# Products of two experts' weight tiles queued directly one behind the other on TensorE

## The chip, the cores and the metric

The kernel runs on one core of a Trainium2 chip. The metric is the time of one execution on the device in microseconds (us), lower is better. The kernel before takes 4514.1 us in the median of three runs (4512.46 to 4516.55).

## What is computed

The reference is two transformer blocks behind each other on 512 tokens of width 1024. The first block (a state-space branch, dilated and memory attention, and a PEER layer) and the token mixers of the second are not touched by the change. The second block has two layers, and each ends with a mixture of experts: of 32 experts each token is sent to two, chosen inside one of four groups, and each expert is a SwiGLU of hidden width 512.

```python
def hier_moe(h, w_grp, b_grp, w_exp, b_exp, w1, w3, w2):
    ...
    def expert_block(args):
        tok_b, w_b, e = args
        xb = t[tok_b]
        hid = jax.nn.silu(xb @ w1[e]) * (xb @ w3[e])
        return (hid @ w2[e]) * w_b[:, None].astype(t.dtype)
```

## The kernel before

The expert stage of a layer (`moe`) gives each expert 64 places for tokens. Its work goes in 17 blocks. In 15 of them two experts share a block of 128 places, 64 each; the other two (`FULL`) hold one expert with 128 places. A block does the following on TensorE:

- `gather` (L1739): products with a one-hot matrix bring the tokens of the block's places into the tile `xg`.
- `hidden` (L1774): for `w1` and then `w3`, eight slices of the input width are multiplied. A weight tile holds two slices of one expert, 128 x 1024 fp32 values or 512 KB. In a block of two experts each product has 64 stationary columns. Those of the first expert fill the rows 0 to 63 of a PSUM tile `acc`, which are the first half of TensorE's columns, and those of the second expert the rows 64 to 127, the second half.
- ScalarE's silu and VectorE's product (L1780, L1781), four transposes on TensorE (L333) and a copy (L1785) make the operand of the next step.
- `rows` (L1796): four weight tiles of `w2` for each expert, again two products of each. ScalarE and VectorE write the result in two parts, `yr` (L1801, L1802).
- `combine` (L1820): products with the one-hot matrix bring the rows of the blocks back to the tokens, and VectorE adds them to `x` (L1822).

Small products with the gate weights (L1835) and transposes of the one-hot matrix (L333) lie in between. One step of `hidden` or `rows` loads a weight tile for each of the two experts, the first expert's first, and makes four products from the two tiles. They are written in the order first expert, second expert, first, second:

```python
for k in range(2):
    kk = 2 * q + k
    for i in range(len(es)):
        T.matmul(ps[i * m:(i + 1) * m], ...
```

Each product is one fp32 matmul of the program, and the trace records it as two passes. Products of gathers and combines have one pass.

All weight tiles go through SyncE's queue (L1759) into a ring of 20 buffers (`RAW`); a transfer waits until the products of the buffer's last tile are through. Six tiles of the first blocks go into other tiles that lie free then (`early`).

The code doesn't fix the order on an engine. When the program is built, a scheduler with a time model of its own places the instructions of all engines, and may put those of a gather or a combine between the products of a step. `tc.issue_after(ins)` adds an edge to that scheduling: what is written inside it comes behind `ins` on the engine of `ins`. It is no wait on the chip.

A loop for tokens that find no place in the blocks (`For_i`) calls `hidden` and `rows` too.

Of the kernel before, what the change touches and what calls it, by code (L numbers as in the profile page):

```python
# [219 lines left out]
class Kernel:  # L220
# [1480 lines left out]
    def moe(self, l):  # L1701
        V, A, P, T, Q = self.V, self.A, self.P, self.T, self.Q
        I = self.I
        tc, nc = self.tc, self.nc
# [3 lines left out]
        with self.pool("mo") as p:  # L1708
# [47 lines left out]
            def weight(src):  # L1756
                i = next(loads)
                w = early[i] if i in early else self.raw.tile([128, 1024], F32, name="raw")
                Q.dma_start(w, src)  # L1759
                return w  # L1760

            def hidden(xg, o, es, fill=iter(())):


                pab = []
                m = 128 // len(es)
                for n in range(2):
                    ps = self.ps("acc", [128, 512])
                    for q in range(4):
                        w = [weight(src(n, q)) for src in es]  # L1770
                        for k in range(2):
                            kk = 2 * q + k
                            for i in range(len(es)):
                                T.matmul(ps[i * m:(i + 1) * m], lhsT=xg[:, kk, o + i * m:o + (i + 1) * m],  # L1774
                                         rhs=w[i][:, k * 512:(k + 1) * 512], start=kk == 0, stop=kk == 7)
                        next(fill, None)
                    pab.append(ps)
                h2 = p.tile([128, 2, 512], F32, name="h2", bufs=2)
                hs, hh = h2[:, 0], h2[:, 1].rearrange("p (k t) -> p k t", k=4)
                A.activation(hs, pab[0], AF.Silu)  # L1780
                V.tensor_mul(hs, hs, pab[1])  # L1781
                tr = self.ps("t", [128, 4, 128])
                for k in range(4):
                    self.transpose(tr[:, k], hs[:, nat(k)])
                A.activation(hh, tr, AF.Copy)  # L1785
                return hh

            def rows(hh, gs, es, fill=iter(())):

                po = [self.ps("acc", [128, 512]) for _ in range(2)]  # L1790
                m = 128 // len(es)
                for f in range(4):
                    w = [weight(src(2, f)) for src in es]
                    for h in range(2):
                        for i in range(len(es)):
                            T.matmul(po[h][i * m:(i + 1) * m], lhsT=hh[:, f, i * m:(i + 1) * m],  # L1796
                                     rhs=w[i][:, h * 512:(h + 1) * 512], start=f == 0, stop=f == 3)
                y = p.tile([128, 2, D], F32R, name="yr", bufs=2)
                for h in range(2):
                    sl = slice(h * 512, (h + 1) * 512)  # L1800
                    A.activation(y[:, 0, sl], po[h], AF.Copy, scale=gs)  # L1801
                    self.end = V.scalar_tensor_tensor(y[:, 1, sl], po[h], gs, y[:, 0, sl].bitcast(F32),  # L1802
                                                      op0=ALU.mult, op1=ALU.subtract)
                return y
# [22 lines left out]
            def expert(ix):  # L1827
                e = Q.value_load(ix, min_val=0, max_val=NEXP - 1)
                return lambda n, q: I[f"{names[n]}_{l}"][bass.ds(e, 1), q].rearrange("o p f -> p (o f)")

            def block(oh, xg, o, col, es, fill):

                pg = self.ps("s", [128, 2])[:, :len(es)]
                for c in range(NT):
                    T.matmul(pg, lhsT=oh.bitcast(F32)[:, c, o:o + 128], rhs=gates[:, c, col:col + len(es)],  # L1835
                             start=c == 0, stop=c == NT - 1)
                gs = p.tile([128, 1], F32, name="gs", bufs=3)
                m = 128 // len(es)
                for i in range(len(es)):
                    V.tensor_copy(gs[i * m:(i + 1) * m], pg[i * m:(i + 1) * m, i:i + 1])  # L1840
                t = slot_major(oh, o)
                hh = hidden(xg, o, es, fill)
                fill = yield
                yield rows(hh, gs, es, fill), t
# [27 lines left out]
            for i, col in enumerate(blocks):  # L1872
                last = i == len(blocks) - 1
                if i == 0 or i % 2:
                    _run(more)
                    oh, xg = nxt
                es = first
                if i:
# [6 lines left out]
                    es = [expert(ix[:, j:j + 1]) for j in range(1 if i in FULL else 2)]  # L1885
# [18 lines left out]
            with tc.For_i(0, n, 1) as i:  # L1904
                ohs = [onehot(128, FAR, j) for j in range(2)]
                pg = self.ps("s", [128, 1])
                for j in range(2):
                    for c in range(NT):
                        T.matmul(pg, lhsT=ohs[j].bitcast(F32)[:, c], rhs=wts[:, j, c:c + 1], start=j + c == 0, stop=j + c == NT)
                gs = p.tile([128, 1], F32, name="gs", bufs=3)  # L1910
                V.tensor_copy(gs, pg)
                V.tensor_add(ohs[0], ohs[0].bitcast(F32), ohs[1].bitcast(F32))
                xg = p.tile([128, KC, 128], F32, name="xg", tag="b8", bufs=2)
                _run(gather(ohs[0], xg))
                t = slot_major(ohs[0], 0)
                es = [expert(order[0:1, bass.ds(i * 2 + NEXP + j, 1)]) for j in range(2)]
                hh = hidden(xg, 0, es)
                _run(combine([(rows(hh, gs, es), t)], True))
                V.tensor_scalar(slots, slots, -128.0, None, op0=ALU.add)
                self.rms_stat(again=True)  # L1920
# [219 lines left out]
```

## Time and profile before

| | |
|---|---|
| median of three runs | 4514.1 us |
| the profiled execution | 4515.67 us |
| its span, first to last instruction | 4513.8 us |
| TensorE busy | 4287.2 us (95%) |
| VectorE, ScalarE, GpSimd busy | 2741.7, 1454.2, 1226.3 us (61%, 32%, 27%) |
| passes of 128 x 64 x 512 of L1774 and L1796 | 497 + 223 us busy, without those of early tiles |
| mean granted TensorE clock | 0.974 of full speed |

The profile is one execution. Busy time is the time in which an engine has at least one instruction under way. Passes on TensorE are pipelined and their ends are modelled, so their durations overlap; what a pass occupies is read from the distance between starts. The expert stages of the two layers lie at about 2752 to 3332 us and 3906 to 4488 us of the span.

### The profile page before, as it was taken

Reading aid. Unit: us, or ns where it says so; the run is one execution under the profiler, and the core shown is the slowest. Engines: PE = TensorE matmul, PEld = TensorE weight load, DVE = VectorE, ACT = ScalarE, POOL = GpSimd, SP = SyncE. Lnnn points to the kernel's source line nnn. Section 1 sums busy time; section 2 is a strip of 40 time slices with the busy share of each in tenths; the row PEclk is TensorE's granted clock in tenths of the full one; section 3 lists DMA queues with packets and bytes.
Section 4 is the critical chain, followed back from the end, with each engine's and each line's share of the span. In section 5 each row is a group of like instructions: output and inputs, shape, how many; then the busy total and the mean of one; then the engine's idle time right before and its main releaser. Section 6 shows DMA issues by size and latency. Waiting matters only on the chain. (4 is left out here: it accounts for less than half of the span.)

```text
span 4513.8 us, 60036 instructions
## 1 busy us (share of the span) xinstructions
PE 4287.2 (95%) x21607; PEld 3269.0 (72%) x21607; DVE 2741.7 (61%) x5347; ACT 1454.2 (32%) x2579; POOL 1226.3 (27%) x883
## 2 busy tenths in 40 slices
PE   8998989998999989999999998999989999899997
PEld 7777777898999989999877774454458778554443
DVE  6577776699998888995458855222234655522122
ACT  5324442344566533333333321000023433200001
POOL 2153336007543344440123540000010445100000
PEclk9999999999999999999999998999999999899999
DMA  4133433347999999994334437988952122698985
GB/s 154 54 99 109 130 109 115 111 139 265 343 354 348 353 347 323 333 321 150 133 92 135 146 117 277 401 319 293 370 189 80 58 68 96 233 369 319 346 315 235
DMA packets 351619, 987.42 MB, mean 219 GB/s; under 512 B 34289, under 2 KB 114673, under 8 KB 349393
## 3 DMA queue, kind: packets, MB, share of 16 engines
q1 hardware_dynamic: 293488, 795.77, 49.6%
q0 software_dynamic: 39392, 162.55, 9.9%
q10 hardware_dynamic: 18432, 25.17, 1.5%
q8 instruction: 174, 2.85, 0.3%
q14 instruction: 133, 1.08, 0.1%
HBM read 926.70 MB, written 56.66 MB: 218 GB/s over the span
## 5 line engine op out<-in xcount | busy, mean ns | idle before, releaser
L267 ACT ACTIVATE whi<-raw 128x1024 fp32r<-128x1024 f32 (+3 forms) x582 | 567.8, 978 | 1168.7 <-PE acc L273 678.3
L268 DVE TENSOR_TENSOR wlo<-raw,whi 128x1024 fp32r<-128x1024 f32 (+4 forms) x438 | 537.2, 1231 | 232.4 <-ACT whi L267 225.4
L1774 PE MATMUL acc<-raw,xg 128*64 128x512 f32 (+1 forms) x2024 | 554.6, 599 | 0.0
L274 PE MATMUL acc<-hn_hi,wlo 128*128 128x384 f32 (+1 forms) x1152 | 397.6, 346 | 15.2 <-DVE wlo L268 15.0
L272 PE MATMUL acc<-hn_hi,whi 128*128 128x384 f32 (+1 forms) x1152 | 401.0, 349 | 2.9 <-ACT act L1141 2.7
L273 PE MATMUL acc<-hn_lo,whi 128*128 128x384 f32 (+1 forms) x1152 | 396.9, 344 | 0.0
L349 POOL TENSOR_TENSOR ssq<-ssq,sq 128x512 f32<-128x512 f32 (+1 forms) x22 | 31.4, 1442 | 1336.9 <-ACT sq L348 1336.8
L268 POOL TENSOR_TENSOR wlo<-raw,whi 128x1024 fp32r<-128x1024 f32 (+3 forms) x144 | 280.3, 1948 | 377.2 <-ACT whi L267 372.3
L1774 PEld LDWEIGHTS acc<-raw,xg 128*64 128x64 f32 (+1 forms) x2024 | 164.0, 140 | 283.6 <-issue 261.1
L272 PE MATMUL acc<-c_hi,whi 128*128 128x384 f32 x1024 | 348.3, 341 | 10.9 <-ACT c_hi L267 5.2
L274 PE MATMUL acc<-c_hi,wlo 128*128 128x384 f32 x1024 | 346.4, 340 | 9.6 <-DVE wlo L268 9.6
L273 PE MATMUL acc<-c_lo,whi 128*128 128x384 f32 x1024 | 347.6, 340 | 0.2 <-DVE c_lo L268 0.2
L1822 DVE SCALAR_TENSOR_TENSOR x<-t,mod,x 128x512 f32<-128x512 f32 x160 | 117.4, 749 | 250.0 <-PE t L1820 250.0
L463 DVE RECIPROCAL gate<-gate 128x512 f32<-128x512 f32 x72 | 240.9, 3346 | 35.5 <-POOL gate L462 35.4
L1073 POOL DMA_INDIRECT rows<-in_rows_up_dram,ridx x128 | 179.6, 1403 | 283.9 <-DVE racc L1086 226.1
L1796 PE MATMUL acc<-raw,h 128*64 128x512 f32 (+1 forms) x1000 | 251.5, 597 | 3.9 <-ACT h L1785 3.9
L274 PEld LDWEIGHTS acc<-hn_hi,wlo 128*128 128x128 f32 x1152 | 217.0, 189 | 24.7 <-DVE wlo L268 20.0
L1073 POOL DMA_INDIRECT rows<-in_rows_down_dram,ridx x128 | 173.0, 1352 | 201.4 <-DVE ract L1077 97.7
L272 PEld LDWEIGHTS acc<-hn_hi,whi 128*128 128x128 f32 x1152 | 217.6, 189 | 9.0 <-ACT act L1141 3.3
L273 PEld LDWEIGHTS acc<-hn_lo,whi 128*128 128x128 f32 x1152 | 217.4, 189 | 4.9 <-issue 0.2
L272 PE MATMUL acc<-h_hi,whi 128*128 128x512 f32 x512 | 213.3, 417 | 0.3 <-ACT whi L267 0.3
L272 PEld LDWEIGHTS acc<-c_hi,whi 128*128 128x128 f32 x1024 | 195.3, 191 | 13.5 <-ACT whi L267 7.2
(672 smaller groups left out, 9611.1 us busy)
## 6 DMA issues: line engine op xcount, KB each, us to landing
raw<-in_w_dram SPq DMA_DIRECT2D x756, 512.0 KB, 7.6
raw<-in_down_dram SPq DMA_DIRECT2D x128, 512.0 KB, 5.8
raw<-in_up_dram SPq DMA_DIRECT2D x128, 512.0 KB, 6.1
raw<-in_ada_dram SPq DMA_DIRECT2D x96, 512.0 KB, 3.8
raw<-in_w_gate_dram SPq DMA_DIRECT2D x72, 512.0 KB, 3.4
actd<-act ACTq DMA_DIRECT2D x128, 192.0 KB, 5.5
gd<-gst POOLq DMA_DIRECT2D x12, 2048.0 KB, 11.2
at<-actd SPq DMA_DIRECT2D x30, 768.0 KB, 7.1
```

What stands on the lines that cost most here:

```text
L267: self.A.activation(hi, src, AF.Copy)
L268: (self.P if engine == "ap" else self.V).tensor_sub(lo, src, hi.bitcast(F32))
L272: T.matmul(out, lhsT=l[0], rhs=r[0], start=start, stop=False)
L273: T.matmul(out, lhsT=l[0], rhs=r[1], start=False, stop=False)
L274: self.last = T.matmul(out, lhsT=l[1], rhs=r[0], start=False, stop=stop)
L349: (eng or (self.V if k % 2 else self.P)).tensor_add(self.ssq[k % 2], self.ssq[k % 2], sq)
L463: V.reciprocal(d, d)
L1073: P.indirect_dma_start(r, None, self.I[n], bass.IndirectOffsetOnAxis(ap=st["idx"][:, kk:kk + 1], axis=0))
L1774: T.matmul(ps[i * m:(i + 1) * m], lhsT=xg[:, kk, o + i * m:o + (i + 1) * m], rhs=w[i][:, k * 512:(k + 1) * 512], start=kk == 0, stop=kk == 7)
L1796: T.matmul(po[h][i * m:(i + 1) * m], lhsT=hh[:, f, i * m:(i + 1) * m], rhs=w[i][:, h * 512:(h + 1) * 512], start=f == 0, stop=f == 3)
L1822: V.scalar_tensor_tensor(self.x[:, k], ps, mod[:, 40 + k:41 + k], self.x[:, k], op0=ALU.mult, op1=ALU.add)
```

## The change

The four products of a step are queued as one run. A new helper, `tied`, takes a list of products and puts an `issue_after` edge from each to the next, so that the scheduler keeps them in the order of the list. The list starts, for each slice, with the product of the second expert, whose tile is loaded later. The conditions for start and stop of the accumulation are written in another form with the same values. Nothing else is changed; the lines behind the new helper move down by up to seven (L1774 is now L1779, L1796 is L1801, L1820 is L1827, L1835 is L1842).

```diff
+            def tied(products):
+
+                ins = None
+                for product in products:
+                    with tc.issue_after(ins.ins) if ins is not None else contextlib.nullcontext():
+                        ins = product()
+
...
                         w = [weight(src(n, q)) for src in es]
-                        for k in range(2):
-                            kk = 2 * q + k
-                            for i in range(len(es)):
-                                T.matmul(ps[i * m:(i + 1) * m], lhsT=xg[:, kk, o + i * m:o + (i + 1) * m],
-                                         rhs=w[i][:, k * 512:(k + 1) * 512], start=kk == 0, stop=kk == 7)
+
+                        tied([lambda k=k, i=i: T.matmul(
+                            ps[i * m:(i + 1) * m], lhsT=xg[:, 2 * q + k, o + i * m:o + (i + 1) * m],
+                            rhs=w[i][:, k * 512:(k + 1) * 512], start=q + k == 0, stop=q + k == 4)
+                            for k in range(2) for i in range(len(es))[::-1]])
                         next(fill, None)
...
                     w = [weight(src(2, f)) for src in es]
-                    for h in range(2):
-                        for i in range(len(es)):
-                            T.matmul(po[h][i * m:(i + 1) * m], lhsT=hh[:, f, i * m:(i + 1) * m],
-                                     rhs=w[i][:, h * 512:(h + 1) * 512], start=f == 0, stop=f == 3)
+                    tied([lambda h=h, i=i: T.matmul(
+                        po[h][i * m:(i + 1) * m], lhsT=hh[:, f, i * m:(i + 1) * m],
+                        rhs=w[i][:, h * 512:(h + 1) * 512], start=f == 0, stop=f == 3)
+                        for h in range(2) for i in range(len(es))[::-1]])
```

In the following lists a row is a line of code, the operation, the tile written and the tiles read, and the size; `x4` are four instructions behind each other. First TensorE in layer 0, behind the `rows` products of one block (from about 2906 us of the trace on), where combine products (`t`) and gather products (`s`) stand between the `hidden` products of the next. Before:

```order
L1796 MATMUL acc<-raw,h_25585 64x512 x16
L1820 MATMUL t<-oht,yr 128x512
L1774 MATMUL acc<-raw,xg 64x512
L1820 MATMUL t<-oht,yr 128x512 x3
L1739 MATMUL s<-oh,ht_hi 128x256
L1774 MATMUL acc<-raw,xg 64x512 x4
L1739 MATMUL s<-oh,ht_lo 128x256
L1739 MATMUL s<-oh,ht_hi 128x256
L1739 MATMUL s<-oh,ht_lo 128x256
L1774 MATMUL acc<-raw,xg 64x512 x2
L1820 MATMUL t<-oht,yr 128x512
L1774 MATMUL acc<-raw,xg 64x512
```

After:

```order
L1801 MATMUL acc<-raw,h_25585 64x512 x12
L1827 MATMUL t<-oht,yr 128x512 x2
L1801 MATMUL acc<-raw,h_25585 64x512 x4
L1827 MATMUL t<-oht,yr 128x512 x2
L1739 MATMUL s<-oh,ht_hi 128x256
L1779 MATMUL acc<-raw,xg 64x512 x4
L1739 MATMUL s<-oh,ht_lo 128x256
L1739 MATMUL s<-oh,ht_hi 128x256
L1739 MATMUL s<-oh,ht_lo 128x256
L1739 MATMUL s<-oh,ht_hi 128x256
L1779 MATMUL acc<-raw,xg 64x512 x4
L1827 MATMUL t<-oht,yr 128x512 x2
```

Single `hidden` products between combine products are now part of runs of four, and the combine products stand in twos.

The second place is TensorE in layer 0, in the `rows` products of the last pair ahead of the second full block (from about 3119 us of the trace on). Before:

```order
L1796 MATMUL acc<-raw,h_26829 64x512 x2
L1739 MATMUL s<-oh,ht_lo 128x256
L1739 MATMUL s<-oh,ht_hi 128x256
L1739 MATMUL s<-oh,ht_lo 128x256
L1796 MATMUL acc<-raw,h_26829 64x512 x2
L1739 MATMUL s<-oh,ht_hi 128x256
L1796 MATMUL acc<-raw,h_26829 64x512 x2
L1739 MATMUL s<-oh,ht_lo 128x256
L1835 MATMUL s<-gates,oh 128x2 x2
L1796 MATMUL acc<-raw,h_26829 64x512 x2
```

After:

```order
L1801 MATMUL acc<-raw,h_26829 64x512 x4
L1739 MATMUL s<-oh,ht_hi 128x256
L1739 MATMUL s<-oh,ht_lo 128x256
L1739 MATMUL s<-oh,ht_hi 128x256
L1739 MATMUL s<-oh,ht_lo 128x256
L1842 MATMUL s<-gates,oh 128x2
L1801 MATMUL acc<-raw,h_26829 64x512 x4
L1842 MATMUL s<-gates,oh 128x2 x3
L1801 MATMUL acc<-raw,h_26829 64x512 x4
```

Runs of two products of one expert are now runs of four products of two. In the whole program there are 202 such groups of products with 64 columns before, 124 of them with an odd number of products, and 158 groups after, 4 of them odd. Six groups before and six after, four odd and none, stand in the two loops for overflow.

## Rows read from the trace of the kernel before

**Rows 1.** The page's first line: the span and the number of instructions.
```profile
span 4513.8 us, 60036 instructions
```
**Rows 2.** Busy time by engine in both expert stages; then granted clock, DMA share, GB/s.
```profile
2752.00:3332.00 580.00, 569.76 (x2589) 263.45 (x2588) 149.46 (x299) 57.87 (x94) 3.38 (x3) 1.00 0.85 326
3906.00:4488.00 582.00, 571.52 (x2600) 264.66 (x2600) 151.02 (x310) 58.09 (x94) 3.00 (x3) 1.00 0.85 325
```
**Rows 3.** Waits of TensorE's weight loads, 2752 to 3332: us in total, times, longest.
```profile
PEld acc L1774 <- DMA raw<-in_w_dram: 7.4, 23, 0.4
```
**Rows 4.** Waits of SyncE's queue that issues the weight tiles, 2752 to 3310.
```profile
SPq L1759 <- PE acc L1774: 134.0, 128, 4.6
SPq L1759 <- PE acc L1796: 132.3, 67, 12.1
```
**Rows 5.** TensorE in order of time: start, duration in us, line, tiles, form, passes.
```profile
2912.90 0.51 PE L1820 MATMUL t<-oht,yr 128*128 128x512 f32 x1
2913.33 1.07 PE L1774 MATMUL acc<-raw,xg 128*64 128x512 f32 x2
2914.34 0.96 PE L1820 MATMUL t<-oht,yr 128*128 128x512 f32 x3
...
2915.35 1.94 PE L1774 MATMUL acc<-raw,xg 128*64 128x512 f32 x8
2917.22 0.39 PE L1739 MATMUL s<-oh,ht_lo 128*128 128x256 f32 x1
...
2917.77 1.08 PE L1774 MATMUL acc<-raw,xg 128*64 128x512 f32 x4
2918.78 0.49 PE L1820 MATMUL t<-oht,yr 128*128 128x512 f32 x1
...
2920.20 0.96 PE L1820 MATMUL t<-oht,yr 128*128 128x512 f32 x3
2921.10 1.07 PE L1774 MATMUL acc<-raw,xg 128*64 128x512 f32 x2
...
2925.07 1.93 PE L1774 MATMUL acc<-raw,xg 128*64 128x512 f32 x6
2926.93 0.39 PE L1739 MATMUL s<-oh,ht_hi 128*128 128x256 f32 x1
```
**Rows 6.** The same view, two products of the same half.
```profile
3118.80 1.93 PE L1796 MATMUL acc<-raw,h 128*64 128x512 f32 x4
3120.66 0.50 PE L1820 MATMUL t<-oht,yr 128*128 128x512 f32 x1
```
**Rows 7.** Passes of L1774, then of L1796, in the first expert stage: busy us (passes).
```profile
2752.00:3332.00 580.00, 278.19 (x1024) 82.38 (x1024) 1.00 0.85 326
2752.00:3332.00 580.00, 127.30 (x512) 41.49 (x512) 1.00 0.85 326
```
**Rows 8.** TensorE in order of time, an unbroken run of products.
```profile
2813.99 7.09 PE L1796 MATMUL acc<-raw,h 128*64 128x512 f32 x32
2820.91 13.90 PE L1774 MATMUL acc<-raw,xg 128*64 128x512 f32 x64
2834.74 0.38 PE L1739 MATMUL s<-oh,ht_lo 128*128 128x256 f32 x1
```
**Rows 9.** Weight tiles, 2752 to 3332: time from issue to landing.
```profile
DMA to landing us min/median/max: 3.4/7.5/11.0
```
**Rows 10.** Waits of TensorE's products for other engines, 2752 to 3332.
```profile
PE t L333 <- DVE h L1781: 3.5, 4, 0.9
PE t L1820 <- ACT yr L1801: 2.3, 3, 0.8
```
**Rows 11.** As rows 2, the first two of the slices with the highest DMA share.
```profile
2850.00:2900.00 50.00, 50.00 (x250) 24.25 (x246) 13.86 (x27) 3.77 (x6) 0.00 (x0) 1.00 1.00 393
3250.00:3300.00 50.00, 47.37 (x179) 17.54 (x176) 12.97 (x18) 4.21 (x7) 0.00 (x0) 1.00 1.02 403
```

## Prediction for the changed kernel, made before it ran

> **What bounds the kernel now.** I read the profile from the coarse to the fine. The profiled execution took 4515.67 us, of which the span is 4513.8 us [rows 1]. The changed lines run in two stretches alone, the expert stages of the two layers, so the first view is the busy time in these stretches: from 2752 to 3332 us and from 3906 to 4488 us [rows 2]. TensorE is busy for 570 of 580 us and for 572 of 582 us, at the full granted clock of 1.00 (2.4 GHz), while VectorE and ScalarE stay under a third. The one other resource that is near its limit is the DMA, with a share of 0.85.
>
> Which of the two sets the pace is told by the waits. TensorE's weight loads of the first two projections waited for a weight tile's landing 23 times, 7.4 us in all and never over 0.4 us [rows 3]. The other way round, the queue that issues the weight tiles waited 134.0 and 132.3 us for products of L1774 and L1796 to give back a buffer [rows 4]. The transfers stand behind TensorE, so time that TensorE saves in these stretches should be time that the kernel saves, until the transfers catch up.
>
> The third view is the order of time on TensorE [rows 5]. A product of one expert is 64 columns wide and is recorded as two passes. One row with x4 is two products, one for each half of the columns. What matters is the distance from a row's start to the next row's start: x4 takes 2918.78 - 2917.77 = 1.01 us and x8 takes 2917.22 - 2915.35 = 1.87 us, so two further products cost 0.86 us, or 0.43 us for each step in which both halves work. But x2, one product alone, takes 2914.34 - 2913.33 = 1.01 us, as much as two; and x6 takes 2926.93 - 2925.07 = 1.86 us, as much as x8. The half of the columns that has no product stands idle for two steps. A partner there would cost nothing. A second form of this are two products of the same half: the x4 at 3118.80 takes 1.86 us instead of 1.01 [rows 6].
>
> **The change, part by part.** *Pairs.* The expert stages hold 512 + 256 products in each layer, which the trace shows as 1024 and 512 passes [rows 7]; 48 of these products are of full blocks and 128 columns wide. This count is used up by the main blocks, so the loop for overflow does no pass and is left out below. In the order of before, TensorE's products of 64 columns stand in 202 groups between other work, 6 of them in the two loop bodies: 196 run. Of these, 120 hold an odd number of products, with one too many of one half, and 12 (such as those of [rows 6]) hold two products of the same half. Both halves together count 120 + 24 = 144 products without a partner. In the order of after 152 groups run, and 4 products stand without a partner (two in each layer, where the scheduler still puts combine products between the two). Each product without a partner takes 0.86 us where its part in a pair is 0.43 us. The change saves 140 x 0.43 = 60.2 us.
>
> *Changes of width.* Each visit to a group costs something at its edges. A group x4 is two steps of 0.43 us and takes 1.01 us up to the next row, so 0.15 us is lost in and after it [rows 5]. On the other side, one product of L1820 between two groups takes 2913.33 - 2912.90 = 0.43 us, and three take 2921.10 - 2920.20 = 0.90 us [rows 5], that is 0.235 us for each further one, and 0.195 us for coming and going. A round trip costs 0.15 + 0.195 = 0.345 us. There are 196 - 152 = 44 fewer of them: 15.2 us.
>
> *The rest.* No instruction of the computation is added or removed, and the edge that ties two products is one of the order alone, not a wait on the chip. ACT's and GpSimd's orders don't change at all, VectorE's in a few places by one or two positions. SyncE's queue moves some loads of an expert's number by one or two weight tiles. I put this at nothing, covered by the lead of the weights: a tile is asked for when one of 20 buffers falls free and is used some 19 tiles later; at the fastest, two tiles in four steps, 0.86 us each, that is 16 us, and the slowest landing took 11.0 us [rows 9]. If that cover were gone, the second rival below has the price. The longest unbroken row of products, 96 passes from 2813.99 to 2834.74 us, takes 20.75 us, which is 48 steps and the edge: TensorE drew there at its full rate and waited for no tile [rows 8]. That row stands in the order of after too, and no row there is longer.
>
> *What is late next.* The waits of TensorE for the chain of a block (products, silu, transposes) stay: before, four transposes in a layer came straight behind the products and waited 3.5 us in all, and three combine products waited 2.3 us for their rows [rows 10]. In the order of after I find the same four places with nothing between.
>
> **Sum.** 60.2 + 15.2 = 75.4 us, about 37.7 us in each layer. 4515.67 - 75.4 = 4440.3 us. The median of the runs, 4514.1 us, is 1.6 us below the profiled execution; with that the forecast is 4438.7, given as 4439 us.
>
> *A rule weighed.* The rows show two products of different halves starting together: four passes take two steps. The Trainium skill ("TensorE: Matmul & The Clock Gate", Part 3, The mechanism) says that matmuls start and end strictly in program order. The two passes of one product would then be one step apart, the partner could only overlap the second of them, and a group of k products would take k + 1 steps. The trace does not agree: x8 would take 5 steps, over 2.1 us, and took 1.87.
>
> **The rivals.**
>
> *The weights become the bound.* In five slices of 50 us (one at 2850, one at 3250, two from 4000, one at 4400) the DMA share is already 1.00 to 1.02 [rows 11]. By the order of time these hold some 45 of the 144 products without a partner and some 50 of the 196 groups. If nothing is won there, 45 x 0.43 = 19.4 us of the pairs' gain and 50/196 of the edges' 15.2 us, 3.9 us, are lost: 4439 + 23 = 4462 us. Against it speak the 266 us for which the queue waited for TensorE, and the room in the whole: 384 tiles in a layer at the 403 GB/s of the fullest slice are 1.30 us each, 499 us, against 542 us that remain of the stretch.
>
> *The cover of the chains goes.* If gathers and combines, now kept out of the fours, fell away from the ends of the blocks, all 17 blocks of a layer would show the wait of 0.88 us before the transposes (3.5 / 4) and that of 0.77 us before the combine (2.3 / 3): 2 x (13 x 0.88 + 14 x 0.77) = 44.4 us more, 4483 us. The order of after speaks against it.
>
> *Strict order.* If passes started strictly in the order of the program, a group of k products would take k + 1 steps before and after, and the gain would be one step for each of the 44 groups that go, one for each of the 12 groups of one half, and the edges: 56 x 0.43 + 15.2 = 39.3 us, 4475 us. The rows with x8 and x4 contradict it [rows 5]. This is what the page's rule, above, would make of the change.
>
> *Slower: the later tile first.* Each four now begins with the product of the tile that was asked for last, and the one whose tile is there stands behind it. Where TensorE runs at the front of the landings, each four waits for one more landing, 1.30 us at 403 GB/s [rows 11]. There are 360 fours (12 in each of 15 blocks and 2 layers). From 75.4 / 1.30 = 58 such waits on the kernel is slower. The five full slices, 250 of 1162 us, hold some 77 of them; if all waited, 100 us would be added, and with their own gain lost the time would be 4462 + 100 = 4562 us. The waits of at most 0.4 us [rows 3] put TensorE far from that front.
>
> *No change.* The pairs run as told, but each stretch ends when something else does, and what is saved comes back as waits at the blocks' ends: 4514 us. A TensorE that is busy for 98% of the stretches leaves little room for this.
>
> **How the numbers follow.** Forecast 0.80 (4427 to 4452 us: the sum with some microseconds for waits that come or go and for counts that I took from an order); weights 0.09 (around 4462); chains 0.03; strict order 0.02; slower 0.03; no change 0.03. The range goes from 4427 into the rival of the weights, to 4464 us, and leaves out under 2 in 10. A measurement of this kernel tells 0.2%, 9 us, from no change. All but the last two cases are faster by more: faster 0.94, same 0.03, slower 0.03.
>
> **What the profile after would show.** In both expert stretches nearly all rows of L1779 and L1801 on TensorE have a multiple of four passes, and x4 keeps taking 1.01 us. The stretches shrink from 580 and 582 us to about 543 and 545; everything before 2752 us stays, and the stretch between the layers keeps its length. The queue's waits for buffers fall and the DMA share rises from 0.85 to about 0.91. I am wrong if weight loads wait for landings by more than some 10 us in a layer, if fours stretch beyond 0.86 us plus edges, or if waits before the transposes multiply.

## The result, and the profile after

The changed kernel takes 4437.9 us in the median of four runs (4432.29 to 4448.68), against 4513.84 us before: a ratio of 0.9834, with a 95% interval from 0.9814 to 0.9854. The forecast was 4439 us. The profiled execution took 4435.62 us.

The busy time by engine in the two expert stages shows where the time went (columns as in [rows 2]: the stretch, its length, TensorE's products, weight loads, VectorE, ScalarE, GpSimd, granted clock, DMA share, GB/s). I cut the stretches from the first product of two experts to just behind the last combine product:

```profile
2746.00:3287.00 541.00, 532.91 (x2589) 253.54 (x2588) 148.92 (x299) 57.98 (x93) 2.96 (x3) 1.00 0.90 349
3865.00:4406.00 541.00, 533.17 (x2591) 253.58 (x2589) 149.13 (x305) 57.74 (x93) 2.71 (x3) 1.00 0.90 349
```

They are 39 and 41 us shorter than in [rows 2], with about as many instructions on each engine. From the start of the first such product to the start of the last combine product it was 578.5 and 578.6 us before, and is 540.0 and 540.0 us now: 77.1 us less in both together. The span lost 80.0 us (4513.8 to 4433.8). The other 2.9 us are not the change's: the first stage began at 2746.0 us instead of 2752.0, although no instruction ahead of it had moved, and 3.2 us came back between the stages and at the end. In the kernels of the experiments below, all equal up to there, this start lies anywhere between 2746 and 2759 us. I therefore compare the two stages below, beside the medians.

TensorE in order of time, at the place of the first list of instructions ahead of the prediction:

```profile
2901.44 0.73 PE L1827 MATMUL t<-oht,yr 128*128 128x512 f32 x2
2902.10 1.94 PE L1801 MATMUL acc<-raw,h 128*64 128x512 f32 x8
2903.97 0.73 PE L1827 MATMUL t<-oht,yr 128*128 128x512 f32 x2
2904.54 0.28 PE L1739 MATMUL s<-oh,ht_hi 128*128 128x256 f32 x1
2904.75 1.94 PE L1779 MATMUL acc<-raw,xg 128*64 128x512 f32 x8
2906.62 0.39 PE L1739 MATMUL s<-oh,ht_lo 128*128 128x256 f32 x1
```

Both rows of products are x8, four products, and from start to next start they take 1.87 us, as the x8 of [rows 5] did. In both stages no group with an odd number of products is left, with one exception in each layer, where combine products still came between the products of a four. There a product alone costs what it cost before, 3164.59 - 3163.58 = 1.01 us:

```profile
3163.58 1.07 PE L1779 MATMUL acc<-raw,xg 128*64 128x512 f32 x2
3164.59 0.73 PE L1827 MATMUL t<-oht,yr 128*128 128x512 f32 x2
3165.25 1.07 PE L1779 MATMUL acc<-raw,xg 128*64 128x512 f32 x2
3166.25 0.73 PE L1827 MATMUL t<-oht,yr 128*128 128x512 f32 x2
```

The queue of the weight tiles now waits less for TensorE (118.5 + 90.1 us in the first stage, 266.3 us in [rows 4]) and more for its own earlier transfers. After, and the last of the three lines as it was before:

```profile
SPq L1759 <- PE acc L1801: 118.5, 59, 12.0
SPq L1759 <- PE acc L1779: 90.1, 81, 4.2
SPq L1759 <- DMA raw<-in_w_dram: 86.3, 123, 1.8
```

```profile
SPq L1759 <- DMA raw<-in_w_dram: 69.2, 101, 1.6
```

TensorE's weight loads wait about as little for landings as in [rows 3]; with those of L1801 it is 9.0 us in the first stage, against 8.5 us before:

```profile
PEld acc L1779 <- DMA raw<-in_w_dram: 6.7, 21, 0.8
```

The waits of TensorE's products in the first stage: the four in front of the transposes are those of [rows 10], to the tenth; the three combine products that waited for their rows (2.3 us) are no longer in the list:

```profile
PE t L333 <- DVE h L1788: 3.5, 4, 0.9
PE acc L1801 <- ACT h L1792: 1.9, 6, 0.7
PE t L1827 <- DVE x L1829: 1.3, 3, 0.8
```

### The profile page after: what moved, and what is told of

Read it like the earlier page. It is cut to its first block, busy times and chain, and to the rows that moved or that the text cites. A ratio compares the mean times of both kernels' runs of the same rounds, so it can differ in the third digit from the quotient of the medians.

```text
span 4433.8 us, 60039 instructions
## 1 busy us (share of the span) xinstructions
PE 4213.2 (95%) x21607; PEld 3248.8 (73%) x21607; DVE 2741.1 (62%) x5347; ACT 1454.3 (33%) x2579; POOL 1225.8 (28%) x883
## 5 line engine op out<-in xcount | busy, mean ns | idle before, releaser
L1779 PE MATMUL acc<-raw,xg 128*64 128x512 f32 (+1 forms) x2024 | 497.1, 598 | 0.0
L272 PE MATMUL acc<-c_hi,whi 128*128 128x384 f32 x1024 | 348.5, 341 | 10.9 <-ACT c_hi L267 5.3
L1779 PEld LDWEIGHTS acc<-raw,xg 128*64 128x64 f32 (+1 forms) x2024 | 152.4, 140 | 268.9 <-issue 251.6
L1801 PE MATMUL acc<-raw,h 128*64 128x512 f32 (+1 forms) x1000 | 240.8, 597 | 3.9 <-ACT h L1792 3.9
```

What stands on the lines that cost most here:

```text
L272: T.matmul(out, lhsT=l[0], rhs=r[0], start=start, stop=False)
L1779: tied([lambda k=k, i=i: T.matmul(ps[i * m:(i + 1) * m], lhsT=xg[:, 2 * q + k, o + i * m:o + (i + 1) * m], rhs=w[i][:, k * 512:(k + 1) * 5 ...
L1801: tied([lambda h=h, i=i: T.matmul(po[h][i * m:(i + 1) * m], lhsT=hh[:, f, i * m:(i + 1) * m], rhs=w[i][:, h * 512:(h + 1) * 512], start=f ...
```

## The experiments

All were run beside the kernel before, whose median was 4514.7 us beside the first four of them and 4516.6 us beside the other four (four each, eight each and fewer buffers); times from the two sets compare to about 2 us. Numbers of groups and of products without a partner are read from the order of each kernel, without the loops.

### The edges without the turned order, and the turned order without the edges

First, the lists start with the first expert's product again; the edges stay.

```diff
-                            for k in range(2) for i in range(len(es))[::-1]])
+                            for k in range(2) for i in range(len(es))])
...
-                        for h in range(2) for i in range(len(es))[::-1]])
+                        for h in range(2) for i in range(len(es))])
```

> The edges of tied stay, but each list starts with the first expert's product, as before the change. In the order of this kernel 190 groups of 64-column products run and 124 products stand without a partner (before: 196 and 144; after: 152 and 4). If products without a partner and round trips set the gain (0.43 us and 0.345 us each), this kernel takes 120 x 0.43 + 38 x 0.345 = 64.7 us more than after: about 4503 us, 0.998 of before. If what counts is that the edges keep four products in the order of the list, whatever its first one is, it takes 4438 us like after.

It took 4506.1 us, 0.9983 of before (0.997 to 0.9995). Second, the turned order stays and the edges go.

```diff
-                    with tc.issue_after(ins.ins) if ins is not None else contextlib.nullcontext():
+                    with contextlib.nullcontext():
```

> Only the order in which the products are written is changed (second expert first); the edges of tied are left out. Every engine's order comes out row for row as in after. The theory of partners expects the time of after, 4438 us, within a few us. If the edges did something on the chip that the order does not show, it would lie nearer to before, 4514 us.

It took 4440.6 us, 0.9848 of before (0.9825 to 0.987). The two stages of the first, then of the second:

```profile
2756.00:3328.00 572.00, 564.61 (x2592) 261.59 (x2592) 150.01 (x303) 57.73 (x93) 2.67 (x3) 1.00 0.87 330
3908.00:4480.00 572.00, 564.66 (x2592) 261.55 (x2592) 149.35 (x299) 57.68 (x92) 2.50 (x3) 1.00 0.86 330
```

```profile
2751.00:3292.00 541.00, 532.73 (x2588) 253.36 (x2586) 148.98 (x299) 58.12 (x93) 3.15 (x3) 1.00 0.91 349
3870.00:4411.00 541.00, 533.17 (x2591) 253.70 (x2589) 149.19 (x305) 57.74 (x93) 2.70 (x3) 1.00 0.91 349
```

The second is the kernel after, row for row in its order and to the microsecond in its stages (541 and 541 us). The first lies 3 us from what its 124 products without a partner and its 190 groups said. So writing the second expert's product first brings the whole gain by itself, and the edges add nothing to it. Without the turned order they brought 16 of the 77 us in the stages. An edge fixes who comes before whom, not that nothing comes between. Why the turned order suffices I did not isolate; it fits the scheduler's model in which the first expert's tile lands first: with its product in front, that product can go while the other tile is still on its way, and something else is put between. With the later tile's product in front, all four can go once the first can. This reading rests on the orders alone.

### One half's products behind each other

The theory has each half of TensorE's columns take its next pass when it is free. How far in the queue may that pass stand from the one in front? In the first of three kernels the four are written as both products of the second expert, then both of the first.

```diff
-                            for k in range(2) for i in range(len(es))[::-1]])
+                            for i in range(len(es))[::-1] for k in range(2)])
...
-                        for h in range(2) for i in range(len(es))[::-1]])
+                        for i in range(len(es))[::-1] for h in range(2)])
```

> Each run of four is written as both products of the second expert, then both of the first, tied. 158 groups run, 54 products stand without a partner in their group, but inside the groups products of one half now stand behind each other. If each half of the columns takes its next pass as soon as it is free, wherever in the group it stands, the four still take four steps of 0.43 us, and the time is that of after plus 50 x 0.43 + 6 x 0.345 = 23.6 us: about 4461 us. If passes started strictly in the order of the program, a four would take seven steps, three more in each of some 360 fours: over 400 us more, about 4900 us.

It took 4470.2 us (0.9908, 0.9892 to 0.9925). Strict order, with several hundred us, is out. A long run of products in this order:

```profile
2822.00 13.95 PE L1779 MATMUL acc<-raw,xg 128*64 128x512 f32 x64
2835.88 1.95 PE L1842 MATMUL s<-gates,oh 128*128 128x2 f32 x16
```

64 passes take 13.88 us, 32 steps of 0.43 us and the edge: full rate. Of the 9 us above the expectation 5 come from three places in each layer where a combine product follows the last `rows` products directly and waits for them, as in the kernel before; after has none. The groups there take 0.9 us more than their steps and edges.

For the other two I started from the kernel with sixteen products in a run (below), and put four, then eight, products of one expert behind each other.

```diff
-                    for q in range(4):
-                        w = [weight(src(n, q)) for src in es]
+                    for q in range(0, 4, 4):
+                        w = [[weight(src(n, q + j)) for src in es] for j in range(4)]
...
-                            rhs=w[i][:, k * 512:(k + 1) * 512], start=q + k == 0, stop=q + k == 4)
-                            for k in range(2) for i in range(len(es))[::-1]])
+                            rhs=w[k // 2][i][:, k % 2 * 512:(k % 2 + 1) * 512], start=2 * q + k == 0, stop=2 * q + k == 7)
+                            for i in range(len(es))[::-1] for k in range(8)])
```

With four each, the three ranges are `range(0, 4, 2)`, `range(2)` and `range(4)`.

> The kernel with sixteen products in a run, but in each half of a projection four products of the second expert stand behind each other, then four of the first (8 passes of one half of the columns, then 8 of the other). 87 groups run, and by count 50 products have no partner in their group. If each half takes its own passes whatever stands between in the queue, the time is that of the sixteen (4421 us) plus 50 x 0.43 + 3 x 0.345 = 22.5 us: about 4443 us. If passes start strictly in the order of the program, only one step of each eight products is shared: 7 steps more in 120 such runs of eight, 361 us more, about 4780 us. A reach that ends between 4 and 16 passes would lie between the two.

> As the run with four each, but all eight products of the second expert in a projection, then all eight of the first (16 passes, then 16). 81 groups run, 116 products have no partner in their group. Halves that take their own passes however far they stand apart: 4421 + 116 x 0.43 - 3 x 0.345 = about 4470 us. Strict order: 15 steps more in each of 60 projections, 387 us more, about 4810 us. If the reach of the queue is the limit, this one loses more than the run with four each does.

They took 4544.4 us (1.0054, 1.0036 to 1.0072) and 4722.6 us (1.0456, 1.0437 to 1.0475): neither of the two pure answers, but the reach that the expectations allowed for. The sixteen products of one projection, x32, in the order second, first, second, first; then with four each; then with eight each:

```profile
2819.04 7.04 PE L1780 MATMUL acc<-raw,xg 128*64 128x512 f32 x32
2826.01 0.38 PE L1739 MATMUL s<-oh,ht_hi 128*128 128x256 f32 x1
```

```profile
2826.85 8.92 PE L1780 MATMUL acc<-raw,xg 128*64 128x512 f32 x32
2835.69 0.38 PE L1739 MATMUL s<-oh,ht_hi 128*128 128x256 f32 x1
```

```profile
2825.74 12.24 PE L1780 MATMUL acc<-raw,xg 128*64 128x512 f32 x32
2837.91 0.39 PE L1739 MATMUL s<-oh,ht_hi 128*128 128x256 f32 x1
```

From start to next start they take 6.97, 8.84 and 12.17 us: 16, 20 and 28 steps of 0.43 us, with the edges. The starts of the single passes within the rows tell why: with eight each, twelve passes start one step apart, then four pairs start together, then twelve again start alone (12 + 4 + 12 = 28). With four each, four passes go alone at the beginning and four at the end. So the other half starts when no more than four passes, two products, of the first half still stand in front of it.

The weight loads, one for each pass, show the same place with eight each. Up to 2830.46 us there is one in a step; then come three, two and two, which with the last single one are the eight of the four pairs:

```profile
2830.46 0.14 PEld L1780 LDWEIGHTS acc<-raw,xg 128*64 128x64 f32 x1 [0.29 <-issue]
2830.89 0.19 PEld L1780 LDWEIGHTS acc<-raw,xg 128*64 128x64 f32 x3 [0.29 <-issue]
2831.32 0.19 PEld L1780 LDWEIGHTS acc<-raw,xg 128*64 128x64 f32 x2 [0.24 <-issue]
2831.75 0.19 PEld L1780 LDWEIGHTS acc<-raw,xg 128*64 128x64 f32 x2 [0.24 <-issue]
```

The first load of the other half comes no earlier than its first pass. Its tile is not what it waits for: in this kernel twelve lone passes are followed by a pair in 46 places, and in 45 of them that load waited for no landing. The 22 runs of 64 passes in each of the two kernels (32 of `rows`, then 32 of `hidden`) all show the same number of steps. Over the 60 projections, 4 and 12 further steps are 103 and 310 us; the stages are 124 and 309 us longer than those of the kernel with sixteen. What sets the reach at four passes, no run here shows.

### Longer runs

Here the gather and combine products that `hidden` draws between its steps are put behind the last product of a projection.

```diff
                 for product in products:
                     with tc.issue_after(ins.ins) if ins is not None else contextlib.nullcontext():
                         ins = product()
+                return ins
...
-                        tied([lambda k=k, i=i: T.matmul(
+                        last = tied([lambda k=k, i=i: T.matmul(
...
-                        next(fill, None)
+                    with tc.issue_after(last.ins):
+                        for _ in range(4):
+                            next(fill, None)
```

> As after, but the gather and combine products that are written between the steps of a projection are put behind its last product by an edge. 84 groups run instead of 152 and no product is without a partner. With 0.345 us for each round trip and 0.43 us for each partner: 68 x 0.345 + 4 x 0.43 = 25.2 us less than after, about 4413 us. If the round trips cost nothing and only partners count, it takes 4436 us. If longer unbroken runs let TensorE catch up with the landings of the weights, weight loads wait and it is slower than after.

It took 4420.95 us, 0.9796 of before (0.978 to 0.9813), the quickest of all kernels here. Its two stages and TensorE's waits in the first:

```profile
2759.00:3288.00 529.00, 523.71 (x2589) 255.23 (x2588) 150.66 (x299) 58.06 (x93) 2.51 (x3) 1.00 0.92 357
3863.00:4393.00 530.00, 524.89 (x2592) 255.27 (x2592) 150.21 (x296) 58.06 (x92) 2.30 (x2) 1.00 0.92 356
```

```profile
PE t L333 <- DVE x L1832: 2.3, 9, 0.3
PE t L1830 <- DVE x L1832: 2.1, 5, 0.8
PE acc L1804 <- ACT h L1795: 0.7, 1, 0.7
```

By the medians it is 17 us quicker than after. From first product to last combine the stages take 528.4 and 529.1 us, 22.5 us less than after in both together, of the 25.2 us expected. The account is less clean than the sum. The groups of two experts' products got 19.7 us shorter, of which some 8 us are the waits in front of the transposes: after had eight, which cost close to 1 us each, and here none is left. With the 4 lone products (1.7 us) off too, 10.3 us are left for the 68 groups that went, 0.15 us each, as the sum has it. Other work lost 10.9 us at its edges, 0.16 us for each trip, but got only 2.8 us shorter, so some 8 us of it came back. Some 5 us of these are waits for VectorE's additions to `x`: combine products, now in longer rows, and transposes wait 4.4 us for them in the first stage, against 1.8 us in after. The rest I did not trace. So a round trip was worth 0.31 us here (0.345 in the sum), the cover of the chains gave 8 us that I had not expected, and other work took as much. Weight loads did not wait more.

### Fewer buffers

After, with `RAW = 14` and with `RAW = 10` instead of 20.

> After, with 14 buffers for weight tiles instead of 20. The scheduler then orders 192 groups and leaves 8 products without a partner: by these terms 40 x 0.345 + 4 x 0.43 = 15.5 us more than after, about 4454 us. If the lead of the transfers is needed (14 buffers cover 13 x 0.86 = 11 us of the quickest draw, about the slowest landing), weight loads begin to wait and it takes some 10 us more, about 4465 us. If after were already held by the transfers, less lead would cost over 30 us: 4485 us or more.

> After, with 10 buffers. 212 groups, 12 products without a partner: by these terms 60 x 0.345 + 8 x 0.43 = 24 us more than after, about 4462 us. The lead is then 9 x 0.86 = 8 us, less than the slowest landing of 11 us: I expect waits of the weight loads for landings in the trace and about 4485 us. No waits and 4462 us would say that the lead of 20 buffers is not needed at all.

They took 4467.7 us (0.9893, 0.9874 to 0.9912) and 4497.4 us (0.996, 0.9944 to 0.9975). The same run of 96 passes (`rows`, then `hidden`) in after, then with ten buffers:

```profile
3188.33 7.09 PE L1801 MATMUL acc<-raw,h 128*64 128x512 f32 x32 [0.25 <-ACT h L1792]
3195.24 13.90 PE L1779 MATMUL acc<-raw,xg 128*64 128x512 f32 x64
```

```profile
3226.94 3.60 PE L1779 MATMUL acc<-raw,xg 128*64 128x512 f32 x16
3230.94 1.94 PE L1779 MATMUL acc<-raw,xg 128*64 128x512 f32 x8 [0.40 <-DMA raw<-in_w_dram]
3233.37 1.94 PE L1779 MATMUL acc<-raw,xg 128*64 128x512 f32 x8 [0.50 <-DMA raw<-in_w_dram]
3236.03 1.94 PE L1779 MATMUL acc<-raw,xg 128*64 128x512 f32 x8 [0.72 <-DMA raw<-in_w_dram]
```

With ten, one four after another waits for its tiles in this run: this is the rival of the weights, made to happen. It shows what it looks like (fours that start 2.4 to 2.7 us apart instead of 1.72) and that after, whose x64 runs through, is not there. In the first stage the products of the kernel with ten waited nine times for a landing, 5.4 us, and in the second 6.4 us. With fourteen they waited once in the first stage, 0.4 us:

```profile
PE t L333 <- DVE h L1788: 7.1, 8, 0.9
...
PE acc L1801 <- DMA raw<-in_w_dram: 0.4, 1, 0.4
```

Its time, 4467.7 us, is near the 4465 us that waits for landings were expected to give, but the trace shows another cause: what made fourteen slower is for the most part the order that the scheduler wrote for fewer buffers. The stages are 26.6 us longer than in after: 15.5 us are more groups and lone products, by the terms of the expectation, and some 7 us are twice as many waits in front of the transposes (7.1 us here, 3.5 us in after). With ten the stages are 53 us longer: 24 us by the same terms, some 11 us more waits in front of the transposes, and 12 us of products waiting for landings. Even there the weights are the smaller part. Both kernels change the order along with the buffers, so they bound the rival and don't size it.

## Why the prediction was right

**What bounds.** The transfers stood behind TensorE, and still do: the queue waits 209 us of a stage for buffers, the DMA share rose to 0.90 (0.91 forecast) and weight loads wait about as before. The stages shrank by 77.1 us, 1.7 us more than the sum's 75.4. That the median lies within 1.1 us of the forecast is in part luck: the four runs are 16 us apart, and the kernel without edges, with the same order, took 4440.6 us. The figure that tests the sum is that of the stages.

**Pairs, 60.2 us, and edges, 15.2 us.** The groups of two experts' products take 721.5 us before and 650.4 us after, added up over their 196 and 152 visits from the first start to the next row's: 71.1 us less. The sum has 60.2 us of partners and 44 x 0.15 = 6.6 us of edges here, 66.8 us. The rest of it, 4.3 us, is the three waits of 0.77 us in each layer before the combine, 4.6 us, which are gone: before, 14 groups took over 0.1 us more than their steps and edges, eight in front of the transposes and these six; after, the eight alone. The prediction had these waits staying, which is the one step of it that failed, and its size is within the range. Outside the groups, the edges of gathers and combines lost 9.0 us, of 44 x 0.195 = 8.6 us in the sum, and other work there took 3 us more, which I did not trace.

**Edits put at nothing.** The prediction took the edges of `tied` for an order and no wait. The kernel without them has the same order and, in the stages, the same time to 0.1 us. The moved loads of an expert's number cost nothing that the waits of the weight loads would show.

**The rivals.** The weights did not become the bound: apart from the eight waits before the transposes, each of the 152 groups of after takes its steps and edge to within 0.1 us, and longer waits for landings came only with ten buffers. The cover of the chains did not go: the same four waits, 3.5 us. Strict order fell by the run of two and two: with two products of each half in turn, 64 passes took 32 steps, which a strict order of starts does not allow. The Trainium skill ("TensorE: Matmul & The Clock Gate", Part 3, The mechanism) says that matmuls start and end strictly in program order. On the starts this trace does not agree, and the measurement decides. The slower case, fours that wait for the later tile, would have shown as in the rows with ten buffers and did not.

## What to carry to other kernels

When products use half of TensorE's columns, read the distance from a group's start to the next row: an odd count costs as much as the next even one, and a group of two products of the same half as much as four. What decides is which two products stand behind each other; where the order is a scheduler's, it can be enough to write the operand that comes last first, so that all of a group are ready together, and an edge that orders them does not keep others out. Look at the order that comes out before trusting either.

## What the runs showed of the hardware

Passes on different halves of the columns started within 60 ns of each other where no more than four passes of one half stood in front of the other in the queue; with eight in front, four went alone, with sixteen, twelve. All these are fp32 passes with 64 stationary and 512 moving columns; no other form was run in this way. The order in which two experts' products are queued gave 4421 us at one extreme and 4723 us at the other, with the same products and nearly the same groups.
